# Storing the last row of a layer-norm + GELU kernel in two transfers, of partitions 0 to 119 and 120 to 127

## Chip, cores, metric

One core of a Trainium2 chip. The metric is the device time of one execution in microseconds (us). Every comparison is made with runs of the kernel before on the same chip, interleaved in rounds.

## The reference

Each of 8 x 1024 = 8192 rows of 2048 float32 values is normalised, scaled by gamma, shifted by beta and put through the tanh form of GELU:

```python
mean = np.mean(x, axis=-1, keepdims=True)
var = np.var(x, axis=-1, keepdims=True)
out = gamma * (x - mean) / np.sqrt(var + eps) + beta
return 0.5 * out * (1 + np.tanh(np.sqrt(2 / np.pi) * (out + 0.044715 * out ** 3)))
```

67 MB are read and 67 MB written, with little arithmetic per byte.

## The kernel before

The rows are cut into 16 blocks of 128 partitions x 4 rows (4 MB). Loads are issued from SyncE, stores from ScalarE. A block is stored in one 4 MB transfer, except the last (`by_row`), whose four rows of 1 MB are stored one by one as each is finished.

```python
xg = xf.rearrange("(b p r) d -> b p r d", p=P, r=R)      # P = 128, R = 4, d = 2048
og = of.rearrange("(b p r) d -> b p r d", p=P, r=R)
...
def by_row(b):
    return b == B - 1
def stored(b):            # what the store semaphore of a slot has reached
    return sum(16 * (R if by_row(c) else 1) for c in range(b) if slot(c) == slot(b))
...                       # ScalarE, per row: normalise, then GELU out of PSUM, then store
ins = ac.activation(out=xt[:, q], in_=pss[i % 2], func=ACT.Gelu_apprx_tanh)._wait_ge(s_t, i + 1)
if by_row(b):
    ins.then_inc(s_r, 1)
    ac.dma_start(out=og[b, :, q:q + 1], in_=xt[:, q:q + 1])._wait_ge(
        s_r, b + q + 1).then_inc(s_store[slot(b)], 16)
    ac.sem_inc(s_g, 1)
...                       # SyncE, at the end
for b in range(B, B + SLOTS):
    sy.wait_ge(s_store[slot(b)], stored(b))
```

Of the kernel before, what the change touches and what calls it, by code (L numbers as in the profile page):

```python
# [10 lines left out]
R = 4  # L11
# [6 lines left out]
def kernel(  # L18
# [9 lines left out]
    P = 128  # L28
# [10 lines left out]
    og = of.rearrange("(b p r) d -> b p r d", p=P, r=R)  # L39
# [28 lines left out]
    def sem(name):  # L68
        return tc.alloc_semaphore(name)
# [3 lines left out]
    s_store = [sem(f"store{s}") for s in range(SLOTS)]  # L73
# [10 lines left out]
    s_r = sem("r")  # L84
# [4 lines left out]
    def slot(b):  # L89
        return (b + SLOTS - 1) % SLOTS  # L90

    def row(p):
        return rows[p:p + 1, :, :d // K]

    def split(v):
        return v.rearrange("o (k f) -> o k f", k=K)
# [4 lines left out]
    def by_row(b):  # L101
        return b == B - 1

    def stored(b):
        return sum(16 * (R if by_row(c) else 1) for c in range(b) if slot(c) == slot(b))

    with tc.tile_critical(), nc.Block() as block:  # L107

        @block.sync
        def _(sy):  # L110
            for b in range(B):
                s = slot(b)
                if stored(b):
                    sy.wait_ge(s_store[s], stored(b))
                for q in range(R):
                    if b == 0:
                        sy.dma_start(out=xts[s][:, q:q + 1], in_=xg[0, :, q:q + 1]).then_inc(s_first[q], 16)
                    elif b == SPLIT:
                        sy.dma_start(out=xts[s][:, q:q + 1], in_=xg[b, :, q:q + 1]).then_inc(s_load[s], 16)
                if b not in (0, SPLIT):  # L120
                    sy.dma_start(out=xts[s], in_=xg[b]).then_inc(s_load[s], 16 * R)

            for b in range(B, B + SLOTS):
                sy.wait_ge(s_store[slot(b)], stored(b))
# [59 lines left out]
        @block.scalar  # L184
        def _(ac):
            ac.preload_act_table(ACT.Gelu_apprx_tanh)  # L186
            for k, (p, src) in enumerate(((64, gamma), (0, beta), (32, beta))):
                ac.dma_start(out=row(p), in_=src.rearrange("(o k f) -> o k f", o=1, k=K)).then_inc(s_par[k], 16)
            ac.wait_ge(s_m, 1)
            ac.activation(out=split(b_hl[0:1]), in_=row(0), func=ACT.Identity)._wait_ge(s_par[1], 16).then_inc(s_c, 1)  # L190
            ac.activation(out=split(b_hl[32:33]), in_=row(32),  # L191
                          func=ACT.Identity)._wait_ge(s_par[2], 16).then_inc(s_c, 1)
            ac.activation(out=g_t, in_=pss[0], func=ACT.Identity)._wait_ge(s_tg, 1).then_inc(s_c, 1)  # L193
            for t in range(T + 1):
                if t < T:
                    b, q = divmod(t, R)
                    ac.activation(out=yks[t % 2], in_=xts[slot(b)][:, q], func=ACT.Identity, scale=rss[:, q:q + 1],  # L197
                                  bias=nms[:, q:q + 1])._wait_ge(s_p, t + 1).then_inc(s_n, 1)
                i = t - 1
                if i < 0:  # L200
                    continue
                b, q = divmod(i, R)
                xt = xts[slot(b)]
                ins = ac.activation(out=xt[:, q], in_=pss[i % 2], func=ACT.Gelu_apprx_tanh)._wait_ge(s_t, i + 1)  # L204
                if by_row(b):
                    ins.then_inc(s_r, 1)
                    ac.dma_start(out=og[b, :, q:q + 1], in_=xt[:, q:q + 1])._wait_ge(  # L207
                        s_r, b + q + 1).then_inc(s_store[slot(b)], 16)
                    ac.sem_inc(s_g, 1)
                elif q == R - 1:  # L210
                    ins.then_inc(s_r, 1)
                    ac.dma_start(out=og[b], in_=xt)._wait_ge(s_r, b + 1).then_inc(s_store[slot(b)], 16)
                    ac.sem_inc(s_g, 1)
                else:
                    ins.then_inc(s_g, 1)
# [65 lines left out]
```

## Time and profile before

| | before |
|---|---|
| time, median of the first 3 runs | 320.58 us (320.54 to 320.70) |
| span of the profiled run | 318.6 us |
| mean DMA rate over the span | 421 GB/s |
| busiest compute engine (ScalarE) | 79% |
| last store issued | 308.94 us |
| 15 DMA engines done / the 16th to finish done | 314.47 / 316.40 us |
| end of the span | 318.58 us |

The last five rows are times in the trace from the start of the span. The profile lines that carry them are in the prediction below. The kernel is bound by its DMA engines (at 90% or more in 38 of 40 slices of the span); at the very end one of them works about 1.9 us longer than the rest.

### The profile page before, as it was taken

To read this page: it belongs to the slowest core of one execution; us is meant where nothing else is said; L and a number is where in the kernel's file an instruction comes from. 1 tells how busy PE (TensorE), PEld (TensorE's weight loads), DVE (VectorE), ACT (ScalarE), POOL (GpSimd) and SP (SyncE) were. 2 spreads that over 40 slices of the span, in tenths; PEclk is the share of its full clock that TensorE was granted. 3 is DMA by queue.
4 is the path that set the end of the run, shared out by engine and by line. 5 is a ranking of instruction groups with operands and counts; after the bars stand their busy time and mean duration, and the time that the engine had idled before them with its cause. 6 is when DMAs were issued, how large, how long until landed. Compare 5 with 4: busy or idle time off the path is not lost.

```text
span 318.6 us, 2087 instructions
## 1 busy us (share of the span) xinstructions
PE 244.4 (77%) x520; PEld 57.2 (18%) x520; DVE 247.5 (78%) x386; ACT 251.7 (79%) x132; POOL 110.5 (35%) x201
## 2 busy tenths in 40 slices
PE   2769999999999989686895868959688795867840
PEld 1212122222222212111221211212121121111100
DVE  4499999999999997896869968698786978859610
ACT  2769999999999989697796958959598696976860
POOL 1144444444444444233333333243232442324300
DMA  7999999999999999999999999999999999999994
GB/s 289 438 457 403 381 452 424 448 411 448 428 432 444 412 453 407 453 436 424 448 407 453 420 436 444 416 453 407 453 432 428 444 411 453 411 444 440 420 410 186
DMA packets 6002, 134.26 MB, mean 421 GB/s; under 512 B 704, under 2 KB 752, under 8 KB 752
## 3 DMA queue, kind: packets, MB, share of 16 engines
q1 hardware_dynamic: 3168, 67.11, 49.4%
q10 hardware_dynamic: 2832, 67.13, 48.9%
q14 instruction: 2, 0.02, 0.0%
HBM read 67.13 MB, written 67.11 MB: 421 GB/s over the span
## 4 chain that ended last, share of the span: by engine, by line
DMA 63%; ACT 14%; DVE 10%; POOL 5%; PE 3%; issue 1%; ACTq 0%; DVEq 0%; POOLq 0%; SPq 0%
DMA out_dram<-xt 31%; DMA xt<-in_x_dram 30%; ACT yk L197 9%; DVE sts L151 7%; ACT xt L204 4%; POOL ves L137 3%; DVE zg L160 2%; PE ps L222 2%; POOL rss L139 2%; DMA rows<-in_gamma_dram 2%; DVE mvs L157 1%; POOL nms L141 1%; PE ps L239 1%; ACT g_t L193 1%; ACTq L207 0%
## 5 line engine op out<-in xcount | busy, mean ns | idle before, releaser
L151 DVE BATCH_NORM_STATS2 sts<-xt 128x6 f32<-128x512 f32 x256 | 157.7, 679 | 32.1 <-DMA xt<-in_x_dram 30.7
L197 ACT ACTIVATE yk<-xt,nms,rss 128x2048 bf16<-128x2048 f32 x64 | 133.7, 2090 | 47.8 <-POOL nms L141 42.3
L239 PE MATMUL ps<-zg,ident 128*128 128x512 bf16 x256 | 120.8, 627 | 54.6 <-DVE zg L160 53.5
L235 PE MATMUL ps<-b_hl,ones_b 33*128 33x512 bf16 x256 | 120.6, 624 | 2.2 <-PEq L230 2.2
L204 ACT ACTIVATE xt<-ps 128x2048 f32<-128x2048 f32 x64 | 118.9, 1857 | 1.5 <-PE ps L239 1.5
L137 POOL TENSOR_SCALAR ves<-mvs 128x1 f32<-128x1 f32 x64 | 37.4, 585 | 177.9 <-DVE mvs L157 177.9
L160 DVE TENSOR_TENSOR zg<-yk,g_t 128x2048 bf16<-128x2048 bf16 x64 | 76.5, 1195 | 19.0 <-ACT yk L197 19.0
L239 PEld LDWEIGHTS ps<-zg,ident 128*128 128x128 bf16 x256 | 27.7, 130 | 147.7 <-DVE zg L160 112.4
L235 PEld LDWEIGHTS ps<-b_hl,ones_b 33*128 33x128 bf16 x256 | 27.0, 127 | 92.1 <-issue 88.4
L139 POOL TENSOR_TENSOR rss<-ves,mhalf 128x1 f32<-128x1 f32 x64 | 37.1, 580 | 5.3
L141 POOL TENSOR_SCALAR nms<-mvs,rss 128x1 f32<-128x1 f32 x64 | 34.9, 546 | 6.3
L157 DVE BATCH_NORM_AGGREGATE mvs<-sts 128x2 f32<-128x24 f32 x64 | 16.9, 264 | 2.2
L222 PE MATMUL ps<-rows,ones 1*128 1x512 f32 x8 | 7.2, 1076 | 5.9 <-DMA rows<-in_gamma_dram 5.9
L190 ACT ACTIVATE b_hl<-rows 1x2048 bf16<-1x2048 f32 x1 | 1.9, 1909 | 5.3 <-DMA rows<-in_beta_dram 5.3
L168 DVE TENSOR_TENSOR b_hl<-rows,b_hl 1x2048 bf16<-1x2048 f32 x1 | 2.3, 2281 | 3.0 <-ACT b_hl L191 3.0
L222 PEld LDWEIGHTS ps<-rows,ones 1*128 1x128 f32 x8 | 2.5, 326 | 9.0 <-DMA rows<-in_gamma_dram 5.9
L193 ACT ACTIVATE g_t<-ps 128x2048 bf16<-128x2048 f32 x1 | 1.9, 1877 | 1.8 <-PE ps L222 1.8
L186 ACT ACT_TABLE_LOAD x1 | 1.3, 1283 | 0.9 <-SPq L107 0.9
L191 ACT ACTIVATE b_hl<-rows 1x2048 bf16<-1x2048 f32 x1 | 1.9, 1908 | 0.0
L163 DVE MEMSET b_hl<- 33x1024 uint32 x1 | 0.9, 912 | 1.2 <-SPq L107 1.2
L128 POOL MEMSET ones<- 65x128 f32 x1 | 0.2, 201 | 0.5 <-SPq L107 0.5
L132 POOL TENSOR_SCALAR_AFFINE_SELECT ident<-ident 128x128 bf16<-128x128 bf16 x1 | 0.3, 292 | 0.1
(7 smaller groups left out, 0.9 us busy)
## 6 DMA issues: line engine op xcount, KB each, us to landing
out_dram<-xt ACTq DMA_DIRECT2D x15, 4096.0 KB, 33.9
xt<-in_x_dram SPq DMA_DIRECT2D x14, 4096.0 KB
xt<-in_x_dram SPq DMA_DIRECT2D x8, 1024.0 KB, 8.2
out_dram<-xt ACTq DMA_DIRECT2D x4, 1024.0 KB, 9.2
rows<-in_beta_dram ACTq DMA_DIRECT2D x2, 8.0 KB, 5.9
rows<-in_gamma_dram ACTq DMA_DIRECT2D x1, 8.0 KB, 4.9
```

Of the source, the lines that this page charges most:

```text
L137: po.tensor_scalar(out=ves[:, c], in0=mvs[:, k, 1:2], scalar1=float(eps), scalar2=1.0, op0=ALU.add, op1=ALU.mult)._wait_ge(s_a, k + 1).the ...
L139: po.tensor_tensor(out=rss[:, c], in0=ves[:, c], in1=mhalf, op=ALU.pow)._wait_ge(s_q, 2 * k + 1).then_inc(s_q, 1)
L141: po.tensor_scalar(out=nms[:, c], in0=mvs[:, k, 0:1], scalar1=rss[:, c], scalar2=-1.0, op0=ALU.mult, op1=ALU.mult)._wait_ge(s_q, 2 * k + 2 ...
L151: ins = ve.bn_stats(out=sts[:, q, j, :], in_=xr[:, j, :])
L157: ve.bn_aggr(out=mvs[:, q], in_=sts[:, q])._wait_ge(s_o, count).then_inc(s_a, 1)
L160: ve.tensor_tensor(out=zgs[q % 2], in0=yks[q % 2], in1=g_t, op=ALU.mult)._wait_ge(s_n, count).then_inc(s_z, 1)
L193: ac.activation(out=g_t, in_=pss[0], func=ACT.Identity)._wait_ge(s_tg, 1).then_inc(s_c, 1)
L197: ac.activation(out=yks[t % 2], in_=xts[slot(b)][:, q], func=ACT.Identity, scale=rss[:, q:q + 1], bias=nms[:, q:q + 1])._wait_ge(s_p, t + ...
L204: ins = ac.activation(out=xt[:, q], in_=pss[i % 2], func=ACT.Gelu_apprx_tanh)._wait_ge(s_t, i + 1)
L222: ins = pe.matmul(pss[0][:, cols(j)], lhsT=ones[64:65], rhs=rows[64:65, j * K // nsub:(j + 1) * K // nsub, :d // K], start=True, stop=True)
L235: ins = pe.matmul(ps[:, cols(j)], lhsT=ones_b, rhs=b_hl[:, cols(j)], start=True, stop=False)
L239: ins = pe.matmul(ps[:, cols(j)], lhsT=ident, rhs=zgs[k % 2][:, cols(j)], start=False, stop=True)
```

## The change

The intent: the DMA engine that ends last is taken to be the 16th. A transfer of 120 partitions is taken to run on 15 engines and one of 8 partitions on 8, so the last row is split such that the 16th engine has nothing of it.

Here a number is an engine's place, counted from 0, in the order in which small transfers take them, and the 16th is the one that the transfer of 120 partitions leaves out.

```diff
     def stored(b):
-        return sum(16 * (R if by_row(c) else 1) for c in range(b) if slot(c) == slot(b))
+        return sum(16 * (R + 1 if by_row(c) else 1) for c in range(b) if slot(c) == slot(b))
...
-                    ac.dma_start(out=og[b, :, q:q + 1], in_=xt[:, q:q + 1])._wait_ge(
-                        s_r, b + q + 1).then_inc(s_store[slot(b)], 16)
+                    for p in (slice(0, P),) if q < R - 1 else (slice(0, 120), slice(120, P)):
+                        ac.dma_start(out=og[b, p, q:q + 1], in_=xt[p, q:q + 1])._wait_ge(
+                            s_r, b + q + 1).then_inc(s_store[slot(b)], 16)
```

## The prediction

> **What bounds the kernel now.** I read the page of the profile first: the slices of the span, then the chain that ended last, then the issues.
>
> ```profile
> DMA  7999999999999999999999999999999999999994
> GB/s 289 438 457 403 381 452 424 448 411 448 428 432 444 412 453 407 453 436 424 448 407 453 420 436 444 416 453 407 453 432 428 444 411 453 411 444 440 420 410 186
> HBM read 67.13 MB, written 67.11 MB: 421 GB/s over the span
> DMA 63%; ACT 14%; DVE 10%; POOL 5%; PE 3%; issue 1%; ACTq 0%; DVEq 0%; POOLq 0%; SPq 0%
> out_dram<-xt ACTq DMA_DIRECT2D x4, 1024.0 KB, 9.2
> ```
>
> The 16 DMA engines are at 90% or more in 38 of 40 slices, while no compute engine passes 79% of the span. The kernel is bound by the bytes that the DMA engines move, and the only slices where they are not full are the first (7 tenths) and the last (4 tenths). The change touches the very last transfer only, so everything is decided in that last slice. The last line is the four row stores at the end, of which the change splits the fourth.
>
> Next, the order of instructions at the end, and the busy time in stretches after the last issue (columns: stretch, length, busy time of each engine, granted clock, mean share of the 16 DMA engines, GB/s).
>
> ```profile
> 307.04 1.88 ACT L204 ACTIVATE xt<-ps 128x2048 f32<-128x2048 f32 x1 [1.48 <-PE ps L239]
> 308.94 0.34 ACTq L207 DMA_DIRECT2D out_dram<-xt  x1
> ```
>
> ```profile
> 309.00:311.50 2.50, 0.00 (x0) 0.00 (x0) 0.00 (x0) 0.00 (x0) 0.00 (x0) 1.00 1.02 429
> 311.50:313.80 2.30, 0.00 (x0) 0.00 (x0) 0.00 (x0) 0.00 (x0) 0.00 (x0) 1.00 1.00 424
> 313.80:314.40 0.60, 0.00 (x0) 0.00 (x0) 0.00 (x0) 0.00 (x0) 0.00 (x0) 1.00 0.30 123
> 314.40:315.00 0.60, 0.00 (x0) 0.00 (x0) 0.00 (x0) 0.00 (x0) 0.00 (x0) 1.00 0.07 27
> 315.00:315.60 0.60, 0.00 (x0) 0.00 (x0) 0.00 (x0) 0.00 (x0) 0.00 (x0) 1.00 0.06 27
> 315.60:316.20 0.60, 0.00 (x0) 0.00 (x0) 0.00 (x0) 0.00 (x0) 0.00 (x0) 1.00 0.06 27
> 316.20:316.40 0.20, 0.00 (x0) 0.00 (x0) 0.00 (x0) 0.00 (x0) 0.00 (x0) 1.00 0.00 0
> 316.40:318.58 2.18, 0.00 (x0) 0.00 (x0) 0.00 (x0) 0.00 (x0) 0.00 (x0) 1.00 0.00 0
> ```
>
> The last store is issued at 308.94 us; the engines are still full with what was queued before it, until 313.80. Then the share falls to 0.06, which is one engine of 16 (1/16 = 0.0625), at 27 GB/s. That one engine works alone from about 314.5 to 316.4. So the tail has a straggler, and it costs about 1.9 us. The packet times in the trace say the same: 15 engines end their part of the last row between 313.89 and 314.48, and one at 316.41. Each share is 8 packets of 8192 B, one per 0.306 us, so 2.45 us. The straggler ends its third row at 313.53, stands still for 0.42 us, and then writes its 8 packets. The increments of the store's semaphore repeat it: 15 land by 314.81, the 16th at 316.86. In the three row stores before it the 16th increment also comes 1.52 us after the 15th, so the lateness was carried along and did not arise in the last row. From the last increment to the end of the span are 1.72 us more, which the change leaves alone.
>
> [...]
>
> **The change part by part.**
> - Removed: the 16th engine's 8 packets of the last row. If it is the straggler, it is done at 313.53, and 316.41 is no longer the end.
> - Added on engines 0-7: one packet of 8192 B each, 0.31 us, and one more semaphore packet (0.009 us). Latest end by packets: between 314.48 (if the latest of the 15 is among engines 8-14) and 314.48 + 0.32 = 314.80. Gain: 316.41 - 314.80 = 1.6 to 316.41 - 314.48 = 1.9; placing the 15 measured start times on the engines at random gives 1.75 on average.
> - Added on the ACT queue: one more issue, 0.34 us as the others take, at about 309.3. The engines have other work until about 311.5, so it lies beside that: 0.
> - The waits at the end: the count for that slot grows by 16 (3 x 16 + 5 x 16 = 128); same single wait: 0.
> - Data, compute and all before 308.94: unchanged.
> Sum if each engine still runs at its 0.306 us per packet: 320.58 - 1.75 = 318.8 us.
>
> **The rivals.**
> [...]
> [...]
> *The straggler is another engine.* If it is among the first 15, it keeps its 8 packets and, if among the first 8[...], gets one more: 320.6 to 320.9.
> *The lateness is not tied to an engine,* but to whatever engine gets some other work. Against: all four row stores have one late increment by 1.5 us or more.
>
> **Range and chances.** I give the clean gain (318.8) 0.45[...], the wrong engine 0.1. Weighted: 0.45 x 318.8[...] + 0.1 x 320.8 = 320.3; I set the point a little lower, at 320.0, since the clean outcome is the most likely single one. Range 318.5 to 322.0: its low end is a gain of 2.1, more than the straggler's whole lateness[...]. Two per cent are 6.4 us; the whole stretch from the last issue to the end of the packets is 7.5 us, so neither a gain nor a loss of that size is in reach. Faster 0.005, within 0.98, slower 0.015.
>
> **What would show it right or wrong.** Clean: the stretch at share 0.06 is gone, packets of the last row keep 0.309 us each, the last packet ends 5.5 to 5.9 us after the (first) last-row issue instead of 7.5, and the end comes 1.7 us after the last increment as before.[...] packets of the last row that take 0.6 us, and a DMA share that stays near 1 while GB/s falls towards 200.[...] Wrong engine: a lone engine at 27 GB/s as before. It would all be wrong if the new issue delays the last data beyond 311.5, or if the time moves with nothing changed after 308.94.

What is cut here: a paragraph of assumptions about the DMA engines, two rivals in which other engines' packets of the last row are slowed, with their times, and what hung on these. The weighted sum came to 320.3 with four terms. Two of them, with the chances 0.35 and 0.1, are cut with their rivals, so the two left (0.45 x 318.8 and 0.1 x 320.8) do not add up to it. Of the first cut rival the signs stand: packets of 0.6 us, and a share near 1 with a falling rate.

## The result, and the profile after

| | before | after |
|---|---|---|
| time, median of 4 runs | 320.64 us (320.54 to 321.05) | 321.30 us (320.59 to 321.76) |
| ratio, 95% interval | | 1.0016 (0.9992 to 1.0040) |

A ratio is the mean time of one kernel's runs over that of the other's of the same rounds, so not quite the ratio of the medians quoted. There is no gain; if anything a loss of 0.2%. The four times lie in two groups, 320.59 and 320.89 against 321.71 and 321.76. The profiled run, 320.59 us, is one of the short ones.

The issues of the changed kernel, from its page, and the last instruction in order of time (start, length, engine):

```profile
out_dram<-xt ACTq DMA_DIRECT2D x1, 960.0 KB
out_dram<-xt ACTq DMA_DIRECT2D x1, 64.0 KB
```

```profile
309.28 1.89 ACTq L208 DMA_DIRECT2D out_dram<-xt  x2
```

The two issues take 1.89 us together (0.60 and 1.26 in the trace), where one took 0.34 before. That is not on the path: the engines are still busy with the third row until 311.3. The stretches of the tail, with the columns of the prediction (stretch, length, five engines' busy time, granted clock, DMA share, GB/s):

```profile
311.50:313.80 2.30, 0.00 (x0) 0.00 (x0) 0.00 (x0) 0.00 (x0) 0.00 (x0) 1.00 0.90 285
313.80:314.40 0.60, 0.00 (x0) 0.00 (x0) 0.00 (x0) 0.00 (x0) 0.00 (x0) 1.00 0.88 314
314.40:315.00 0.60, 0.00 (x0) 0.00 (x0) 0.00 (x0) 0.00 (x0) 0.00 (x0) 1.00 0.67 259
315.00:315.60 0.60, 0.00 (x0) 0.00 (x0) 0.00 (x0) 0.00 (x0) 0.00 (x0) 1.00 0.31 109
315.60:316.20 0.60, 0.00 (x0) 0.00 (x0) 0.00 (x0) 0.00 (x0) 0.00 (x0) 1.00 0.17 68
316.20:316.80 0.60, 0.00 (x0) 0.00 (x0) 0.00 (x0) 0.00 (x0) 0.00 (x0) 1.00 0.03 14
```

From 311.50 to 313.80 the share is still 0.90, but the rate has dropped from 424 to 285 GB/s: packets are in flight for longer. And something still runs after 316.20. The DMA view of the stretch from 316.2 on counts what that is:

```profile
DMA packets 3, 0.01 MB, mean 5 GB/s; under 512 B 2, under 2 KB 2, under 8 KB 2
```

One data packet and two semaphore packets: a single engine that closes one transfer, sends one packet of 8192 B and closes another.

The trace does not number the DMA engines, but it has every packet, and a packet begins within 3 to 6 ns of the end of the one before it on its engine. So packets can be linked into chains, one per engine. In the tail of the kernel before this gives 16 complete chains. Where packets are slowed, gaps of up to some 25 ns occur, and a chain of a timely engine (one that is not late) is then a likely linking, not the only one. Below, a number is a packet's length in us and `|t` a semaphore packet at t, that is, the end of one transfer on that engine. Timely engines can swap places where their times coincide; the late one cannot where it is alone.

```
before, late engine       ... |313.94  0.31 0.31 0.31 0.31 0.31 0.31 0.31 0.31 |316.40
before, a timely engine   ... |311.51  0.31 0.31 0.31 0.31 0.31 0.31 0.31 0.31 |313.96
after,  late engine       ... |313.85  0.31 0.31 0.31 0.31 0.31 0.31 0.31 0.31 |316.30 0.31 |316.61
after,  a timely engine   ... |311.48  0.49 0.84 0.70 0.32 0.55 0.47 0.32 0.40 |315.60 0.31 |315.91
after,  without a last row ... |311.40
```

Three things can be read here. The engine without any of the last row ended its third row at 311.40, among the timely ones (311.3 to 312.8): the engine that was left out, the 16th, was not late; it is so in every trace of such a cut. The late engine still has its 8 packets, and a ninth: it is one of the 8 engines that took the transfer of 8 partitions. And a timely engine's 8 packets now take up to 4.1 us instead of 2.45. The span went from 318.58 to 318.81, by 0.23; of this the late engine's end accounts for 316.61 - 316.40 = 0.21, which is the ninth packet (0.31) less 0.09 by which its third row came sooner.

### The profile page after: what moved, and what is told of

It reads as the page before. It is cut to its first block, busy times and chain, and to the rows that moved or that the text cites. A ratio compares the mean times of both kernels' runs of the same rounds, so it can differ in the third digit from the quotient of the medians.

```text
span 318.8 us, 2088 instructions
## 1 busy us (share of the span) xinstructions
PE 244.3 (77%) x520; PEld 57.2 (18%) x520; DVE 247.5 (78%) x386; ACT 251.7 (79%) x132; POOL 110.8 (35%) x201
## 4 chain that ended last, share of the span: by engine, by line
DMA 63%; ACT 14%; DVE 10%; POOL 5%; PE 3%; issue 1%; ACTq 0%; DVEq 0%; POOLq 0%; SPq 0%
DMA out_dram<-xt 31%; DMA xt<-in_x_dram 31%; ACT yk L197 9%; DVE sts L151 7%; ACT xt L204 4%; POOL ves L137 3%; DVE zg L160 2%; PE ps L223 2%; DMA rows<-in_gamma_dram 2%; POOL rss L139 2%; POOL nms L141 1%; DVE mvs L157 1%; PE ps L240 1%; ACT g_t L193 1%; ACTq L208 0%
```

## Experiments

The theory after the first trace: the late engine is one of the first 8, carries 9 packets instead of 8, and sets the end; slowed packets cost the others 1 to 2 us (8 packets in up to 4.1 us instead of 2.45), hidden behind it. The rivals: the slowed packets set the end; the late engine is the 16th, or another in every run. Where the expectations say "sharing", read slowed packets, over 0.4 us where 0.31 is usual; the traces show that they take longer, not why. Each experiment changes how the last row is cut. Unless said otherwise the edit is this, with a list `LAST` of partition ranges and the semaphore count to match:

```diff
-                    for p in (slice(0, P),) if q < R - 1 else (slice(0, 120), slice(120, P)):
+                    for p in (slice(0, P),) if q < R - 1 else LAST:
-        16 * (R + 1 if by_row(c) else 1)
+        16 * (R - 1 + len(LAST) if by_row(c) else 1)
```

What the traces show of the tail, in us from the start of the span ("rest" is the latest end of the engines other than the late one; the 313.8 is worked back from 315.91 by 7 packets of 0.306; the ladders, e9 and e10 are told in their places):

| kernel | last row issued | late engine: third row ends | its last packet ends | rest ends |
|---|---|---|---|---|
| before | 308.94 | 313.94 | 316.40 | 314.47 |
| changed, first trace | 309.28 | 313.85 | 316.61 | 316.07 |
| changed, second trace | 310.17 | 313.94 | 316.71 | 316.69 |
| changed, third trace (a long run) | 312.01 | none apart | | 318.65 |
| 120 only | 310.22 | 313.99 | 316.44 | 316.37 |
| two halves of 64 | 310.24 | 314.03 | 316.60 | 316.85 |
| 120 + 3 + 3 + 2 | 309.31 | 313.82 | 316.28 | 316.95 |
| 105 + 15 + 8 | 309.98 | 313.8 | 316.53 | 315.64 |
| two column halves | 309.90 | 313.66 | 316.16 | 315.89 |

In the traces of the two halves of 64 and of the column halves a second engine is a row behind (it ends at 316.21 and at 315.89). The late engine is told from it by its packets of 32768 B in the block before the last: eight of them take 9.87 us, those of the second engine 9.68 or 9.69.

### Which engine is late: three ladders (e1_ladder, e5_ladder2, e12_ladder3)

The author's assumption: a transfer of k partitions, k small, runs on the first k engines of one order. How many engines it takes is seen in the packet counts: the trace of e9 (112 partitions and four times 4) has 720 packets of under 512 B, 16 more than the kernel before, so 16 + 4 x 4 semaphore packets for its last row. That they are the first ones of one order is tested by the ladders themselves. If it holds, a ladder of small transfers gives each engine a number of single packets that tells its place.

```diff
+LAST = (slice(0, 112), slice(112, 119), slice(119, 124), slice(124, 127), slice(127, 128))   # e1
+LAST = (slice(0, 112), slice(112, 120), slice(120, 124), slice(124, 127), slice(127, 128))   # e5
+LAST = (slice(0, 112), slice(112, 117), slice(117, 121), slice(121, 125), slice(125, 128))   # e12
```

> The last row is stored in five transfers of 112, 7, 5, 3 and 1 partitions. [...]every engine gets 7 packets of 8192 B, then engine 0 four more, 1 and 2 three, 3 and 4 two, 5 and 6 one, and 7 to 15 none. How many single packets the late engine sends after its 7 names its group.[...] Rival (late engine is 0 to 6): one to four single packets follow, each with a semaphore packet ahead. Rival of the change's author (it is the 16th): also 7 and nothing more, which the changed kernel already speaks against, since there its late engine had 8 packets and one more. If the late engine is a different one in each run, the count here will not fit with the 8 + 1 of the changed kernel.

> The last row in transfers of 112, 8, 4, 3 and 1 partitions. After 7 packets each, engine 0 sends four single ones, 1 and 2 three, 3 two, 4 to 7 one, 8 to 15 none. The first ladder put the late engine on 3 or 4 (two single packets). If it is engine 3 always: two here; engine 4: one; if it was neither and changes from run to run: any other number, none above all.[...]

> The last row in transfers of 112, 5, 4, 4 and 3 partitions: after 7 packets each, engines 0 to 2 send four single ones, 3 three, 4 one, 5 to 15 none. One single packet after the late engine's 7 therefore means engine 4 and no other. My theory after two ladders (two singles in the first, one in the second; only engine 4 has both counts): one. If the late engine is another on this chip: none (5 to 15, the 16th among them), three or four (0 to 3).

Measured, each on a different chip, the late engine's chain:

```
e1    7 packets |316.75 0.31 |317.06 0.31 |317.37     two singles: engine 3 or 4
e5    7 packets |316.03 0.31 |316.34                  one single:  engine 4 to 7
e12   7 packets |316.03 0.31 |316.34                  one single:  engine 4
```

I had expected no single packet in the first; that was wrong. In the first ladder the other engines' counts were four once, three twice, two twice (the late one among them), one twice and none for the rest, exactly as transfers of 7, 5, 3 and 1 packets on the first engines of one order would have it, so the places can be trusted. In the second, two engines' packets met within 6 ns at 316.34 and the linking was first ambiguous. The late engine's semaphore increments there arrive 0.48 us after its packets, the others' 0.34, which speaks for the linking shown; but in the first ladder the late engine's last increments come after 0.34 like the others', so this is no sure mark. The counts settle it: linked as shown they are four once, three twice, two once and one four times, as such an order has it, and linked the other way no engine would have four. Engine 4 is the only one that fits all three; the third ladder alone names it, if the order is taken as given. That it is the same place on three chips is what the counts show. How it falls behind can be seen in the kernel before: its eight packets of 32768 B between 296.68 and 306.56 took 9.88 us, those of each other engine 9.68. Why its packets are slower stays open. The times (321.35, 321.04 and 320.46 us, one run each) were not the object. The second expectation also foretold few slowed packets in a transfer of 112 partitions. That failed: of the packets begun after 311.4, 36 in the second ladder and 31 in the third took over 0.4 us, against 8 in the first.

### The eight-partition transfer taken away (e2_only120), and the changed kernel again (e4_again)

```diff
+LAST = (slice(0, 120),)        # e2: wrong on purpose, 120 to 127 of the last row are never stored
```

> Wrong result on purpose: only partitions 0 to 119 of the last row are stored, the transfer of 120 to 127 is left out. If the changed kernel ends with the late engine's ninth packet (my theory), the late engine now ends 0.31 us earlier than in the changed kernel: its last packet 2.4 us after its third row, as in the kernel before; time about 320.6, a ratio of 1.000 to the kernel before and 0.3 us less than the changed kernel.[...] If the late engine were the 16th, this run would gain 1 us or more.

> The changed kernel unaltered, for its spread (320.59 to 321.76 in four runs) and for a second trace. My theory: again one late engine, whose last packets are 8 of one transfer and one of the next; mean of fast runs 0.2 to 0.6 us over before, ratio 1.0007 to 1.002. If the late engine changes from run to run, the last engine will now have 8 packets only, or the lone stretch will be gone.

Measured on the same chip: without the eight partitions 320.39 us (320.24 to 320.56), ratio to before 0.9991 (0.9978 to 1.0004); the changed kernel 320.93 us (320.50 to 322.89), ratio 1.0026 (1.0003 to 1.0049), two of its six runs at 322.19 and 322.89. So without the small transfer no loss is seen, and with the 16th engine idle there is no gain of 1.6 us either. (Five runs without a long one, over 321.5 us, are weak evidence: at the 6 long runs in 15 that the changed kernel has in all, they would come up by chance about once in thirteen, an estimate.) But the table spoils half of the theory: in these two traces the rest ends 0.02 to 0.07 us before the late engine. Here the last row was issued 0.9 us later than in the first trace, the rest started 0.5 us later, and with its packets slowed it ended together with the late engine. The stretches of the second trace of the changed kernel:

```profile
314.40:315.00 0.60, 0.00 (x0) 0.00 (x0) 0.00 (x0) 0.00 (x0) 0.00 (x0) 1.00 0.93 300
315.00:315.60 0.60, 0.00 (x0) 0.00 (x0) 0.00 (x0) 0.00 (x0) 0.00 (x0) 1.00 0.90 273
315.60:316.20 0.60, 0.00 (x0) 0.00 (x0) 0.00 (x0) 0.00 (x0) 0.00 (x0) 1.00 0.57 191
```

Where the kernel before has one engine at a share of 0.06, on average more than half of the engines are at work up to 316.2. The ninth packet and the slowed packets of the rest are two limits that lie within about half a microsecond of each other (0.54 us in the first trace, 0.02 in the second).

### Slowed packets without a ninth packet (e3_halves, e6_332)

```diff
+LAST = (slice(0, 64), slice(64, 128))                                            # e3
+LAST = (slice(0, 120), slice(120, 123), slice(123, 126), slice(126, 128))        # e6
```

> The last row in two transfers of 64 partitions, each on all 16 engines with 4 packets apiece: every engine has its 8 packets as before and none has a ninth[...]. My theory: many packets of the last row take 0.4 to 0.8 us on the 15 timely engines, the late one runs nearly alone after them and stays near 0.31 each; the end moves by less than 0.4 us, ratio 1.000 to 1.001. Rival[...]: 1 to 2 us later than before, ratio 1.003 to 1.006.[...]

> The changed kernel, but partitions 120 to 127 in three transfers of 3, 3 and 2 on engines 0 to 2, so that the late engine has 8 packets and no ninth. My theory: the late engine ends 2.45 us after its third row as before (about 316.4) without a single packet after it; the sharing engines end at 316.0 to 316.8, so the time is within 0.3 us of the kernel before, ratio 0.999 to 1.001. If the ninth packet on the late engine is not what the changed kernel loses (rival: sharing alone), no gain on the changed kernel's mean, and the last packet is that of an engine with packets of 0.6 us.

The halves: 320.67 us (320.37 to 322.29), ratio 1.0012 (0.9993 to 1.0031). Every engine has 8 packets; the late one ends at 316.60, its packets 0.31 to 0.41 us, yet the rest, whose packets take up to 0.86, ends at 316.85. The cut into three, three and two: 321.00 us (320.75 to 321.68), ratio 1.0014 (1.0000 to 1.0028): the late engine ends at 316.28, with 8 packets and no ninth, and the rest at 316.95. But that last engine has three single packets (from 316.01 to 316.95) after its 8, so this trace does not show the slowing alone: the 8 packets of every timely engine were done by 316.01. Both sit at the edge of what I had put down, or past it. The theory in its first form falls with the halves: slowed packets are not hidden safely, there they set the end without a ninth packet, by 0.25 us in the one trace.

### The ninth packet with fewer slowed packets (e7_105), and a second transfer with neither (e8_cols)

```diff
+LAST = (slice(0, 105), slice(105, 120), slice(120, 128))                         # e7
```
```diff
-                    for p in (slice(0, P),) if q < R - 1 else (slice(0, 120), slice(120, P)):
-                        ac.dma_start(out=og[b, p, q:q + 1], in_=xt[p, q:q + 1])._wait_ge(
+                    for f in (slice(0, d),) if q < R - 1 else (slice(0, d // 2), slice(d // 2, d)):      # e8
+                        ac.dma_start(out=og[b, :, q:q + 1, f], in_=xt[:, q:q + 1, f])._wait_ge(
```

> The last row in 105 partitions (15 engines[...]), 15 (15 engines, one each) and 8 (8 engines, one each). Again the 16th engine has none and the late engine 9 packets[...]. [...]packets of the 105 transfer stay at 0.31 us on all but some four engines, and the timely engines end by about 315.5, 1 us before those of the changed kernel. The late engine then ends alone, 9 packets or 2.75 us after its third row. If the ninth packet sets the end (my theory): about 316.7, time as the changed kernel, ratio 1.000 to 1.002. If sharing sets it (rival): earlier than the changed kernel by 0.5 us or more, ratio below 0.999.

> A control for the second transfer itself: the last row in two halves of its columns, 128 partitions each on 16 engines, 16 packets of 4096 B per engine at about 0.155 us. No sharing, no ninth packet, the second issue stays. My theory: the late engine ends 16 x 0.155 = 2.5 us after its third row, ratio 0.999 to 1.001, and no run over 321.5. If runs of 321.7 to 322.9 come from a second issue of any kind (rival), they turn up here too, one or two in five.

105 + 15 + 8: 320.67 us (320.59 to 321.01), ratio 1.0003 (0.9989 to 1.0016). The late engine ends alone at 316.53, after 7 packets and two single ones, and the rest at 315.64. The stretches:

```profile
315.00:315.60 0.60, 0.00 (x0) 0.00 (x0) 0.00 (x0) 0.00 (x0) 0.00 (x0) 1.00 0.28 109
315.60:316.20 0.60, 0.00 (x0) 0.00 (x0) 0.00 (x0) 0.00 (x0) 0.00 (x0) 1.00 0.03 14
```

The expectation on single packets was too clean: most engines had one or two packets over 0.4 us. But the packets' time above 0.31 us, summed over those that begin after 311.4, falls to 9 us, from 21 in the second trace of the changed kernel. The sum also depends on when the last row is issued: for 120 partitions it is 11 us at 309.3 (the first trace and the cut into three, three and two) and 18 to 21 at 310.2, for 112 partitions 2 us at 309.03 and 10 at 310.1 (the first ladder, and the other two). This run was issued at 309.98 and is rightly set beside the later ones. With the slowing thus reduced, the ninth packet remains, and it costs what a ninth packet costs: 316.53 against 316.40 before, with a third row that ended 0.1 to 0.2 sooner.

Column halves: 320.40 us (320.16 to 320.67), ratio 0.9994 (0.9980 to 1.0007). Two issues (0.34 and 0.97 us), no packet of the last row over 0.18 us, no long run in five. A second transfer as such costs nothing here. Nor is any packet slowed, though the last row was issued at 309.90: of the cuts tried, those of the partitions slow packets (up to 0.88 us in the first trace) and this one of the columns does not. Why, no trace shows.

### The suspected costs four times (e10_allrows)

```diff
-                    for p in (slice(0, P),) if q < R - 1 else (slice(0, 120), slice(120, P)):
+                    for p in (slice(0, 120), slice(120, P)):
-        16 * (R + 1 if by_row(c) else 1)
+        16 * (2 * R if by_row(c) else 1)
```

> The suspected costs four times: all four rows of the last block are stored as 120 and 8. The late engine gets four more packets (1.2 us), the 16th has none of the block. [...]each row takes 4 us instead of 2.45, the last packets are those of sharing engines, the end comes 3 to 7 us after that of the kernel before, ratio 1.010 to 1.022. Up to 3 us of added issue time sit between the rows, but packets then wait in the queues anyway. If sharing costs nothing and only the ninth packets count (rival): about 1.2 us, ratio 1.004.

324.23 us (324.03 to 324.96), ratio 1.0122 (1.0107 to 1.0136): 3.8 us, not the 1.2 of the ninth packets. The last engines to end are ones with slowed packets (as linked, 8 packets from 315.89 to 319.74, 3.85 us, then one more to 320.05). This is not pure: each row's second issue (0.57 to 2.15 us) held ScalarE, so the last row was issued at 314.14. Part of the 3.8 us may be that delay; the run does not tell it from the slowing.

### Relief for engine 4, and a third trace of the changed kernel (e9_k4, e11_again)

```diff
+LAST = (slice(0, 112),) + tuple(slice(112 + r, 128, 4) for r in range(4))        # e9
```

> Relief for engine 4 instead of the 16th: the last row in 112 partitions (16 engines, 7 each) and the other 16 in four transfers of 4 partitions, every fourth one[...]. If engine 4 is the late one, it sends 7 packets and nothing more, and ends 2.15 us after its third row instead of 2.45, about 316.1; engines 0 to 3 have 11 and end by about 315.8; ratio about 0.999 (0.3 us), within the noise of the times and seen in the packets alone. If the late engine is another of 5 to 15: the same; if it is one of 0 to 3: 11 packets, end near 317.3, ratio 1.003.[...]

> The changed kernel once more, on the chip of the three others, for its times beside theirs and a third trace. My theory: late engine with 8 + 1 packets, its end and those of the sharing engines within 0.6 us of each other, mean 0.2 to 1 us over before. Some runs of 321.5 to 323. If the traced run is one of those, the engine that ends last in it tells what makes them: a sharing engine (theory), the late engine (rival), or data that came late (the last issue after 311).

e9: 321.25 us (320.21 to 322.30), ratio 1.0015 (0.9996 to 1.0035). Its trace is a long run of 321.99, in which the late engine is only 0.2 us behind the next: it ends its third row at 314.20. From there it sends 7 packets to 316.35 and nothing more, and the increment comes 0.48 us later (others' 0.33 to 0.37), so it is not one of engines 0 to 3, which fits engine 4, and the relief reached it. But the four engines with 11 packets ended last, at up to 318.02, so nothing was gained: it is no better version.

e11: 320.84 us (320.48 to 322.55), ratio 1.0012 (0.9999 to 1.0026), and its trace is the long run of 322.55. That answers what the long runs are. First the start of the last block's statistics in the chain that ended last, in the kernel before and then in this run:

```profile
283.73 2.48 DVE sts L151 x4
```

```profile
286.79 2.48 DVE sts L151 x4
```

The last load landed 3.06 us later, everything after it followed, and the last row was issued at 312.01 instead of 308.94. In between, the DMA engines ran dry (stretches of the kernel before, then of this run):

```profile
290.00:300.00 10.00, 8.63 (x20) 1.87 (x18) 8.52 (x14) 9.01 (x6) 3.88 (x8) 1.00 0.98 423
```

```profile
290.00:300.00 10.00, 7.93 (x18) 1.96 (x19) 8.96 (x15) 7.71 (x4) 4.64 (x9) 1.00 0.78 334
```

A share of 0.78 instead of 0.98 over 10 us is 2 us of standing still. The late engine, which has a backlog, hardly stands still: 14 engines had ended the block before by 295.62 and waited, it ended at 296.32, and all of these began the next block together, from 296.44 to 296.59. So it catches up, and no engine is far apart any more. All third rows end between 313.69 and 314.29. Then the last row, again in stretches of this run:

```profile
314.40:315.00 0.60, 0.00 (x0) 0.00 (x0) 0.00 (x0) 0.00 (x0) 0.00 (x0) 1.00 1.09 246
315.00:315.60 0.60, 0.00 (x0) 0.00 (x0) 0.00 (x0) 0.00 (x0) 0.00 (x0) 1.00 1.12 205
316.80:317.40 0.60, 0.00 (x0) 0.00 (x0) 0.00 (x0) 0.00 (x0) 0.00 (x0) 1.00 0.93 273
317.40:318.00 0.60, 0.00 (x0) 0.00 (x0) 0.00 (x0) 0.00 (x0) 0.00 (x0) 1.00 0.57 205
```

The share is about 1, the rate about half: 72 packets take over 0.4 us, 30 of them 0.60 to 0.63, twice 0.31. Eight engines end between 318.06 and 318.65. At 0.306 us a packet, 8 packets from 313.8 would have ended at 316.25 (an estimate), which is no later than the late engine's usual 316.40. So such a spell could pass unseen in the kernel before (no trace of it has one): of its 35 runs the longest is 321.34. The changed kernel has 6 of 15 at 321.67 to 322.89; its other nine have a mean of 320.74, against 320.62 for the 35. That the other five long runs are of the same kind is likely, not shown; one was traced. A remark in e9's expectation that long runs should be absent there failed: it has them as well, with 11 packets on four engines and only 25 packets over 0.4 us.

## Why the prediction was right in its range and wrong in its likeliest way

- **Bound by DMA, decided after the last issue, no change of 2% in reach: right.** 321.3 is inside 318.5 to 322.0, and in the first trace the span follows the late engine's last packet to 0.02 us. That the range held is owed to its width, which took in the rivals: the point, 320.0, was a gain, and no gain came.
- **"Removed: the 16th engine's 8 packets of the last row. If it is the straggler ...": this step failed,** and with it the outcome that I had given 0.45. The removed packets belonged to a timely engine, done with its third row at 311.40, so the term of -1.75 us was worth 0. The ladders put the late one at engine 4. Nothing in the trace of before named any engine, and still I gave the author's choice the largest chance.
- **"The straggler is another engine", 0.1:** the right rival, with the right size for the short runs: 320.6 to 320.9 foretold, nine short runs with a mean of 320.74 (0.12 above the kernel before, which is within the scatter of its runs).
- **Slowed packets, the two rivals, 0.35 and 0.1:** the mechanism that they rested on is not shown, so what remains of them is what was measured. The signs of the first are there as described: packets of 0.6 us, share near 1 with the rate at 205 to 285 GB/s. A timely engine's 8 packets take 2.5 to 4.4 us over the three traces, as linked, and in the one of the longer runs (321.7 to 322.9) that was traced there is no late engine to hide behind. Single packets of the last row reach 0.9 us, and in the first trace one of the third row took 1.18, but in the other two traces 0.60 to 0.63 is the commonest length of a slowed one. I treated slowed packets and another straggler as alternatives; they act together, and whichever ends later counts.
- **A misreading that did no harm:** "The straggler ends its third row at 313.53, stands still for 0.42 us" is wrong, and so is the lateness of 1.52 us in the earlier rows. I had sorted the semaphore increments by time and cut them into sixteens, but the late engine's increment for one row comes after the first ones for the next. Linked packet by packet, the late engine ends its third row at 313.94, does not pause, and is 1.9 us behind the last of the others. The 313.53 is a timely engine's last end, so the other 15 end from 313.53 to 314.48, not from 313.89.
- **The second issue: 0 on the path, right**, though the second issue took 0.47 to 1.26 us and not the 0.34 I had worked with. The column halves show that a second issue costs no time.

## What to carry to other kernels

Before work is taken from a straggler, find out which one it is: small transfers whose engine counts differ give the engines different numbers of packets (here 0 to 4 beside the 7), and one or a few traces then name it. A transfer that leaves out an engine also slowed packets of the others here, and where no late engine stood in front that came out as 2.4 us in the one long run traced (318.65 against the estimate of 316.25); 6 of 15 runs were long, by 1.0 to 2.3 us. A tail with one late engine hides delays of about its lateness (here 1.9 us) in all the others, so the slowing of those showed here as a wider spread of times (320.48 to 322.89 over the changed kernel's 15 runs, 320.16 to 321.34 over the 35 of the kernel before), and with all four rows cut as a shift of the median (3.8 us, part of which may be the later issue).

## What else the runs measured

- One engine is late: 1.9 us behind at the end of the kernel before, and engine 4 by the ladders' counts on three chips. Its packets of 32768 B are slower, 9.88 us for eight against 9.68.
- For 120 and 64 partitions packets of most engines go from 0.31 to between 0.4 and 0.9 us, often 0.60 to 0.63; for 105 and 112 it is fewer of them (with the last row issued at about 310, 9 to 10 us of added packet time against 18 to 23). The rate falls with them, to 205 to 285 GB/s where the kernel before has 424.
- The length of an issue by shape, on ScalarE: 0.34 us for 128 or 112 partitions with nothing just ahead, 0.34 to 0.60 for 120, and 0.47 to 2.15 for a transfer of 2 to 8 partitions issued right after another.
